# A recurrent token mixer on one NeuronCore: chunk matrices kept as 64x64 tiles without zero blocks, the triangular inverse from 16x16 blocks with two product levels, and another order of the head pairs

## The chip, the cores and the metric

The kernel runs on one core of a Trainium2 chip. The metric is device time in microseconds (us) of one execution, taken as the median of several. Durations inside the kernel come from one profiled execution; they are read in views of its trace. The engines are named as the profile names them: PE (TensorE matmuls), PEld (its weight loads), DVE (VectorE), ACT (ScalarE), POOL (GpSimd) and SP (the queue that issues DMAs).

## The reference, cut to what matters

The model is a sequence of 512 tokens, width 1024, through ffn1, a token mixer, ffn2 and two more layers. The change touches only the mixer, whose recurrence over time has one 64x64 state per head (8 heads):

```
def wkv7_scan(r, w, k, v, a, b):
    def step(S, inp):
        r_t, w_t, k_t, v_t, a_t, b_t = inp
        sa = jnp.einsum("bhvk,bhk->bhv", S, a_t)
        S = S * w_t[:, :, None, :] + sa[..., None] * b_t[:, :, None, :] + v_t[..., None] * k_t[:, :, None, :]
        y = jnp.einsum("bhvk,bhk->bhv", S, r_t)
        return S, y
...
y = wkv7_scan(rh, heads(decay), kh, vh, -kk, kk * ah)
```

Around it stand projections (`h @ w_in`, in 42 column groups of 128), three small low-rank products (`tanh(xw) @ w_decay_up`, `xa @ w_iclr_up`, `sigmoid(xg) @ w_gate_up`), a short convolution branch, a normalisation of `y` per head, and gated output projections.

## The kernel before, in words

Everything large is a `gemm`: a weight group of 128x1024 is loaded (`raw`), split into a high part `wh` (ACT or DVE) and a low part `wl` (DVE, or loaded from DRAM where ffn1 made it ahead, `put_low`), and multiplied as three products (`mm3`: high x high, high x low, low x high) of 128x128 by 128x512 in fp32r. One group with 8 row tiles is 24 such matmuls into one PSUM tile `pm`.

The recurrence is computed in 8 chunks of 64 tokens. Two heads make a pair; there are four pairs, `pair(j)` for the preparation and `pair_out(j)` for the rest. In the trace the small fp32 matmuls stand as two instructions each and write PSUM tiles named `pw`. The steps for one pair:

- `pair` makes the scaled vectors: `AR` (tile `ar`) holds the a-like and r-like vectors, `BK` (tile `bk`) the b-like and k-like ones. Its three low-rank products read `lora`; the first two use 64 rows of the array each.
- `chunk_ab`: for each of two halves (`tp`) 4 matmuls of 64x128 by 128 columns give a 128x128 matrix in which two chunks' 64x64 blocks stand on the diagonal and the rest is masked to zero with `mS` (`ab`).
- `inverse32`: the inverse of identity minus a strictly triangular 64x64 matrix is found by substitution on its 32x32 diagonal blocks, all at once on DVE: the blocks go through DRAM (`dab`) so that each lands on a partition (`n`), 31 steps of a multiply (`q`, in one or two instructions) and a reduce (into `u`), then back through DRAM (`dtt`) to `TT`.
- `batch` (once for each half): `x` (16 matmuls of 64x64 by 64 columns) and `y` (4 of 64x128 by 128); 6 fp32 transposes; one product level for the off-diagonal 32x32 block (`p1`, `p2`, 8 matmuls of 32x32 each, with `ab` and `TN` in their names); `pd` and `pq` (4 each of 128x128 by 128, `R,TN` and `R,ak`); `pm` (8 of 64x64 by 128 and 8 by 64, `R,aT` and `vT,R`).
- the scan over chunks: six steps, each with two matmuls (`zb,MN`) and two DVE adds into `zb`, a 128x128 state tile with zero blocks; and the outputs `py`: 16 matmuls by 64 columns (`vT,R`) and 7 of 128x64 by 128 (`zb,aT`), all in one PSUM bank.
- normalisation, four transposes, and two POOL products to `yo`.

The order of work is made by a list scheduler (`Rec.schedule`) from modelled costs (`_cost`). It takes the ready operation with the lowest place in the program first, looks up to 800 operations ahead, and on PE it prefers operations of the array shape in use (`choose`): an operation that needs another shape may wait while operations of the same shape are ready within 400 places, up to 3000 ns. The order found is fixed: each engine runs its list. Eight PSUM banks serve all of it, 76 slots of 128x512 hold activations, and 3, 4 and 4 buffers hold `raw`, `wh` and `wl`. At the end of the mixer `w_out_b` needs the results `ys` of all four pairs.

Almost every operation is emitted from one line (551), so views are read by tile names. The functions that the change touches:

Of the kernel before, what the change touches and what calls it, by code (L numbers as in the profile page):

```python
# [17 lines left out]
_PI = 128 * 128 + 128  # L18


def _mats(t, tp):

    return bass.AP(tensor=t.tensor, offset=t.offset + 4 * tp * _PI, ap=[[128, 128], [_PI, 4], [1, 128]])


def _diag(t, r0, nr):

    return bass.AP(tensor=t.tensor, offset=t.offset + r0 * 128, ap=[[32 * 128 + 32, 32], [128, nr], [1, 32]])
# [40 lines left out]
_CST = ["ident", "ones", "bones", "mS", "mST"]  # L69
# [3 lines left out]
_COFF["e32"] = _COFF["mI"] + 64  # L73
_COFF["eps"] = _COFF["e32"] + 256
# [4 lines left out]
def _const_block():  # L79
# [8 lines left out]
        "mS": same & (p < q),  # L88
        "mST": same & (q < p),
# [5 lines left out]
    c[:, _COFF["e32"]:_COFF["e32"] + 256] = np.repeat(np.eye(32).reshape(4, 256), 32, 0)  # L95
# [44 lines left out]
def layout(i):  # L140
# [13 lines left out]
    lo = np.stack([np.concatenate([f("w_decay_up")[0], f("w_iclr_up")[0]], 0), f("w_gate_up")[0]], 1)  # L154
    o["lora"] = np.ascontiguousarray(lo)
# [438 lines left out]
def _cost(o, outs, ins):  # L594
# [4 lines left out]
    if o.eng == "tensor":  # L599
        if o.fn == "matmul":  # L600
# [7 lines left out]
            if not one and m <= 64 and k <= 64:  # L608
                c *= 0.55
        else:  # L610
            o.mode = 128, 128
            c = 60.0
# [31 lines left out]
class Net:  # L644
# [63 lines left out]
    def D(self, p):  # L708

        t = self.rec.tile(self.dp.tile([8, _PI], F32, name=self.nm(p)), "dram", 99, True)  # L710
        return t
# [195 lines left out]
    def _mixer(self):  # L907
# [20 lines left out]
        self.lw = self.wload(self.a["lora"], (128, 2, 512))  # L928


        zero = self.T(shape=(128, 4, 128), p="z")
# [3 lines left out]
        for i in range(2):  # L935
            for tp in range(2):
                nc.sync.dma_start(out=_mats(self.dtt[i], tp), in_=zero)
# [55 lines left out]
        self.pair_out(*p.pop(1))  # L993
        p[3] = pair(3)
# [3 lines left out]
        gates(1, 5)  # L998
        self.pair_out(*p.pop(3))
        gates(5, 8)  # L1000
# [17 lines left out]
    def pair(self, j, rF, kF, vF):  # L1018
# [6 lines left out]
        lwh, lwl = self.lw  # L1025
        cols = slice(j * 128, j * 128 + 128)
        pw = self.P()
        self.mm3(pw, lwh[0:64, 0, cols], lwl[0:64, 0, cols], self.tw[0][0:64], self.tw[1][0:64], True, True)
# [3 lines left out]
        self.mm3(pa, lwh[64:128, 0, cols], lwl[64:128, 0, cols], self.tw[0][64:128], self.tw[1][64:128], True, True)  # L1032
# [3 lines left out]
        self.mm3(pg, lwh[:, 1, cols], lwl[:, 1, cols], self.sg[0], self.sg[1], True, True)  # L1036
# [46 lines left out]
        ab = [self.chunk_ab(AR[tp], BK[tp]) for tp in range(2)]  # L1083
        TTs = self.inverse32(ab, j)
        return j, AR, BK, F, vF, ab, TTs, bon, gF

    def pair_out(self, j, AR, BK, F, vF, ab, TTs, bon, gF):
# [22 lines left out]


        zb = [self.T(shape=(128, 4, 128), p="zb") for _ in range(2)]
        for z in zb:
            G.memset(z, 0.0)
        zc = lambda c: zb[c // 4][:, c % 4]
        st = []
        for tp in range(2):
            st.append(self.batch(AR[tp], BK[tp], BH, dF, vT, tp, ab[tp], TTs[tp]))
        for tp in range(2):
            MT, N, _, _ = st[tp]  # L1120
            for c in range(4):
                cc = 4 * tp + c
                if cc == 7:
                    break
                if cc == 0:
                    for hh in range(2):
                        r = slice(hh * 64, hh * 64 + 64)
                        A.copy(zc(1)[r, r], N[r, 0])
                    continue
                pz = self.W((128, 64))  # L1130
                for hh in range(2):
                    r = slice(hh * 64, hh * 64 + 64)
                    PE.matmul(pz[r], MT[r, c], zc(cc)[r, r], start=True, stop=True)
                for hh in range(2):
                    r = slice(hh * 64, hh * 64 + 64)
                    V.tensor_tensor(zc(cc + 1)[r, r], pz[r], N[r, c], ALU.add)

        py = self.W((128, 4, 128))
        for tp in range(2):
            _, _, QG, Rh = st[tp]  # L1140
            for tt in range(2):
                t = 2 * tp + tt
                for c in range(2):
                    r = slice(c * 64, c * 64 + 64)
                    last = t == 0 and c == 0
                    for hh in range(2):
                        PE.matmul(py[r, t, hh * 64:hh * 64 + 64], QG[hh][r, 1, tt, 0:64],
                                  vT[r, t, hh * 64:hh * 64 + 64], start=hh == 0, stop=last and hh == 1)
                    if not last:
                        PE.matmul(py[r, t], Rh[:, tt, c * 64:c * 64 + 64], zc(2 * t + c), start=False, stop=True)  # L1150

        yv = py.rearrange("p a (h i) -> p (a h) i", h=2)
# [27 lines left out]
        self.ys.append(self.split(o))  # L1180

    def chunk_ab(self, AR, BK):

        V, PE = self.nc.vector, self.nc.tensor
        X = [self.W((128, 2, 128)) for _ in range(2)]
        for tt in range(2):
# [608 lines left out]
```

## Time and profile before

| what | us |
|---|---|
| median of 3 runs | 1911.29 (1911.15 to 1913.51) |
| the profiled execution, its own time | 1912.9 |
| its span, first to last instruction | 1911.1 |
| PE busy in the span | 1867.3 |
| DVE busy in the span | 1334.9 |
| ACT busy in the span | 852.7 |
| POOL busy in the span | 252.5 |

The span is what the trace covers; the profiled execution's own time is 1.8 us longer. PE's busy time counts each matmul from its start to a modelled end, and neighbouring matmuls overlap, so the pace of PE is read from the starts of neighbouring matmuls and not from their durations. The mixer lies between 380 and 800 us from the span's start.

### The profile page before, as it was taken

Reading aid. Unit: us, or ns where it says so; the run is one execution under the profiler, and the core shown is the slowest. Engines: PE = TensorE matmul, PEld = TensorE weight load, DVE = VectorE, ACT = ScalarE, POOL = GpSimd, SP = SyncE. Lnnn points to the kernel's source line nnn. Section 1 sums busy time; section 2 is a strip of 40 time slices with the busy share of each in tenths; the row PEclk is TensorE's granted clock in tenths of the full one; section 3 lists DMA queues with packets and bytes.
Section 4 is the critical chain, followed back from the end, with each engine's and each line's share of the span. In section 5 each row is a group of like instructions: output and inputs, shape, how many; then the busy total and the mean of one; then the engine's idle time right before and its main releaser. Section 6 shows DMA issues by size and latency. Waiting matters only on the chain.

```text
span 1911.1 us, 25539 instructions
## 1 busy us (share of the span) xinstructions
PE 1867.3 (98%) x9756; PEld 1548.5 (81%) x9756; DVE 1334.9 (70%) x2173; ACT 852.7 (45%) x1187; POOL 252.5 (13%) x201
## 2 busy tenths in 40 slices
PE   8999999999999999999999999999999999999998
PEld 6878888878877777788788788788899888888887
DVE  7766655568977873567566567865378985899774
ACT  5333423453333422444334334522245554898671
POOL 3101101212121200411001014220000101000001
PEclk9999999999999999999999999999999999999999
DMA  7898884526633533658878774412221225555552
GB/s 257 280 318 287 303 281 158 150 97 203 190 125 111 157 129 118 221 180 297 284 262 295 271 272 131 127 58 73 84 86 45 67 67 198 184 185 204 198 176 100
DMA packets 128810, 345.36 MB, mean 181 GB/s; under 512 B 32304, under 2 KB 44848, under 8 KB 128688
## 3 DMA queue, kind: packets, MB, share of 16 engines
q1 hardware_dynamic: 128688, 343.74, 53.7%
q8 instruction: 76, 1.25, 0.3%
q14 instruction: 46, 0.38, 0.1%
HBM read 280.25 MB, written 63.44 MB: 180 GB/s over the span
## 4 chain that ended last, share of the span: by engine, by line
PE 71%; DVE 11%; DMA 11%; ACT 3%; issue 2%; POOL 1%; SPq 1%; DVEq 0%; ACTq 0%; POOLq 0%
PE pm L551 67%; DVE wl L551 4%; PE pw L551 4%; DMA low<-wl 3%; DMA raw<-o_in 2%; DVE t L551 2%; ACT wh L551 2%; DMA raw<-ffn_d 1%; DMA raw<-ffn_u 1%; DMA raw<-w_in 1%; DVE l L551 1%; DMA n<-dab 1%; DMA raw<-gw 1%; SPq L551 1%; DVE q L551 1%
## 5 line engine op out<-in xcount | busy, mean ns | idle before, releaser
L551 ACT CAST wh<-raw 128x1024 fp32r<-128x1024 f32 (+1 forms) x334 | 347.2, 1041 | 678.6 <-PE pm L551 300.7
L551 PE MATMUL pm<-xh,wh 128*128 128x512 f32 x1488 | 584.0, 393 | 9.6 <-ACT xh L551 8.0
L551 PE MATMUL pm<-xl,wh 128*128 128x512 f32 x1488 | 584.1, 393 | 1.9 <-DVE xl L551 1.9
L551 PE MATMUL pm<-xh,wl 128*128 128x512 f32 x1488 | 582.6, 392 | 1.8 <-DVE wl L551 1.8
L551 DVE TENSOR_TENSOR wl<-raw,wh 128x1024 fp32r<-128x1024 f32 (+1 forms) x303 | 383.0, 1266 | 212.1 <-DMA low<-wl 103.6
L551 PEld LDWEIGHTS pm<-xh,wh 128*128 128x128 f32 x1488 | 280.3, 189 | 69.2 <-ACT xh L551 9.1
L551 PE MATMUL pm<-h,wh 128*128 128x512 f32 (+1 forms) x844 | 321.5, 385 | 10.0 <-ACT h L551 6.8
L551 PEld LDWEIGHTS pm<-xl,wh 128*128 128x128 f32 x1488 | 280.5, 188 | 62.4 <-DVE xl L551 5.0
L551 PEld LDWEIGHTS pm<-xh,wl 128*128 128x128 f32 x1488 | 280.4, 188 | 61.6 <-DVE wl L551 4.3
L551 PE MATMUL pm<-l,wh 128*128 128x512 f32 (+1 forms) x844 | 322.2, 384 | 2.6 <-DVE l L551 2.5
L551 PE MATMUL pm<-h,wl 128*128 128x512 f32 (+1 forms) x844 | 321.4, 383 | 0.0
L551 POOL TENSOR_TENSOR t<-t,t 128x512 f32<-128x512 f32 x61 | 95.2, 1561 | 942.2 <-DVE t L551 796.1
L551 PEld LDWEIGHTS pm<-h,wh 128*128 128x128 f32 x844 | 158.2, 188 | 44.3 <-ACT h L551 8.5
L551 PEld LDWEIGHTS pm<-l,wh 128*128 128x128 f32 x844 | 158.4, 188 | 36.5 <-DVE l L551 6.5
L551 PEld LDWEIGHTS pm<-h,wl 128*128 128x128 f32 x844 | 158.5, 188 | 29.8
L551 DVE TENSOR_TENSOR t<-pm,rstd 128x512 f32<-128x512 f32 x146 | 98.7, 684 | 19.8 <-PE pm L551 15.8
L551 ACT ACT_TABLE_LOAD x71 | 91.1, 1283 | 21.9 <-DVE s L551 14.9
L551 DVE CAST wh<-raw 128x1024 fp32r<-128x1024 f32 x75 | 54.9, 733 | 50.6 <-PE pm L551 28.7
L551 POOL TENSOR_TENSOR acc<-acc,sq 128x512 f32<-128x512 f32 x42 | 65.6, 1569 | 138.5 <-ACT sq L551 138.1
L551 DVE TENSOR_TENSOR x<-x,pm 128x512 f32<-128x512 f32 (+1 forms) x44 | 27.8, 636 | 68.8 <-PE pm L551 67.3
L551 ACT ACTIVATE t<-t 128x512 f32<-128x512 f32 x100 | 59.8, 626 | 30.5 <-DVE t L551 29.5
L551 DVE TENSOR_TENSOR l<-t,h 128x512 fp32r<-128x512 f32 x84 | 58.7, 706 | 6.3 <-ACT h L551 5.0
(245 smaller groups left out, 2127.5 us busy)
## 6 DMA issues: line engine op xcount, KB each, us to landing
low<-wl SPq DMA_DIRECT2D x106, 512.0 KB, 3.8
wl<-low SPq DMA_DIRECT2D x106, 512.0 KB, 3.7
raw<-w_in SPq DMA_DIRECT2D x76, 512.0 KB, 4.8
raw<-o_in SPq DMA_DIRECT2D x64, 512.0 KB, 4.5
raw<-ffn_g SPq DMA_DIRECT2D x44, 512.0 KB, 4.0
raw<-ffn_u SPq DMA_DIRECT2D x44, 512.0 KB, 5.0
raw<-ffn_d SPq DMA_DIRECT2D x32, 512.0 KB, 5.2
raw<-o_out SPq DMA_DIRECT2D x32, 512.0 KB, 4.6
```

The source lines that it names most:

```text
L551: o.ins = getattr(getattr(self.nc, o.eng), o.fn)(*o.args, **o.kw)
```

## The change

It does this in the mixer; the rest of the program is the same text.

- All chunk matrices become 64x64 tiles: `ab`, `TT`, `TN` are 128 x 8 x 64 (chunk parity on the partition half), without zero blocks. `chunk_ab` has 16 matmuls of 64x64 by 64, `batch` 48 for `x` and `y`, 16 + 16 by 128 for `pd` and `pq`; `batch` treats both halves in one call, stage by stage.
- The substitution runs on 16x16 blocks (`inverse16`): 15 steps, each with one multiply and one reduce; half the DMAs.
- `inverse64` makes the rest with two product levels, each 16 + 16 matmuls of 64x64 by 64, with three 32x32-block transposes of 128x512 on DVE in all, and two copies on ACT.
- The state `zb` is 128 x 8 x 64, so a scan step has one add of 128x64. The outputs go to two PSUM tiles, one for each head: 16 matmuls ahead of the scan, 14 behind it, all 64x64 by 64 columns.
- The low-rank weights are padded to 128 rows, loaded in three pieces and kept in activation slots, no longer in a `wh` and a `wl` buffer.
- The order is pair 0, pair 1, conv 0, pair 2, conv 1, conv 2, out of pair 0, conv 3, pair 3, and so on; four gates stand behind the last `pair_out` in place of three.
- In the scheduler's model a fp32 matmul of 64x64 costs 31 ns (up to 64 columns) or 105 ns, and a transpose 109 ns in place of 60 ns.

```
+_CH = 64 * 64 + 64
...
+            if not one and m <= 64 and k <= 64:
+                c = 31.0 if n <= 64 else 105.0
...
-            c = 60.0
+            c = 109.0
...
-        self.lw = self.wload(self.a["lora"], (128, 2, 512))
+        self.lw = []
+        for i in range(3):
+            raw = self.T()
+            nc.sync.dma_start(out=raw, in_=self.a["lora"][i])
+            self.lw.append(self.split(raw))
...
+        p[0] = pair(0)
+        p[1] = pair(1)
         conv(0)
-        p[0] = pair(0)
+        p[2] = pair(2)
         conv(1)
-        p[1] = pair(1)
         conv(2)
+        self.pair_out(*p.pop(0))
         conv(3)
+        p[3] = pair(3)
         out_a(0)
-        self.pair_out(*p.pop(0))
-        p[2] = pair(2)
-        gates(0, 1)
+        self.pair_out(*p.pop(1))
         out_a(1)
-        self.pair_out(*p.pop(1))
-        p[3] = pair(3)
         out_a(2)
         self.pair_out(*p.pop(2))
         out_a(3)
-        gates(1, 5)
+        gates(0, 4)
         self.pair_out(*p.pop(3))
-        gates(5, 8)
+        gates(4, 8)
...
+        py = [self.W((128, 4, 64)) for _ in range(2)]
+        for t in range(4):
+            for hh in range(2):
                 for c in range(2):
                     r = slice(c * 64, c * 64 + 64)
+                    o = PE.matmul(py[hh][r, t], st[t // 2][2][hh][r, 1, t % 2, 0:64], vT[r, t, hh * 64:hh * 64 + 64],
+                                  start=t == 0, stop=False)
...
+            for hh in range(2):
+                r = slice(hh * 64, hh * 64 + 64)
+                PE.matmul(pz[r], MT[r, c], zb[r, cc], start=True, stop=True).deps.append(o)
+            V.tensor_tensor(zb[:, cc + 1], pz, N[:, c], ALU.add)
+        for cc in (2, 1, 3, 4, 5, 6, 7):
+            t, c = cc // 2, cc % 2
+            for hh in range(2):
+                r = slice(hh * 64, hh * 64 + 64)
+                PE.matmul(py[hh][c * 64:c * 64 + 64, t], st[t // 2][3][r, t % 2, c * 64:c * 64 + 64],
+                          zb[r, cc], start=False, stop=cc > 5)
...
+        for t in range(1, 16):
             p = q[:, 0:8 * t + 8].rearrange("p (r k) -> p r k", r=8)
+            V.tensor_tensor(p, U[:, :, 0:t + 1], n[:, t:t + 1, 0:t + 1].to_broadcast([128, 8, t + 1]), ALU.mult)
             V.tensor_reduce(U[:, :, t:t + 1].rearrange("p r o -> p (r o)"), p, axis=AX.X, op=ALU.add)
...
+    def inverse64(self, ab, TT):
...
+        a16 = self.T(shape=(128, 8, 64), p="a16")
+        nc.tt(a16, ab, self.c("m16", 64).unsqueeze(1).to_broadcast([128, 8, 64]), ALU.mult)
+        for lvl in range(2):
+
+            b = ab if lvl else a16
+            T = self.T(shape=(128, 8, 64), p="TN")
+            V.transpose(out=f(T), in_=f(TT))
+            p1 = self.W((128, 8, 64))
+            for m in range(8):
+                for c in range(2):
+                    k = slice(64 * c, 64 * c + 64)
+                    PE.matmul(p1[k, m], b[k, m], TT[k, m], start=True, stop=True)
+            x1 = self.T(shape=(128, 8, 64), p="XT")
+            A.copy(x1, p1)
+            p2 = self.W((128, 8, 64))
+            for m in range(8):
+                for c in range(2):
+                    k = slice(64 * c, 64 * c + 64)
+                    PE.matmul(p2[k, m], x1[k, m], T[k, m], start=True, stop=True)
...
+            else:
+                V.tensor_tensor(T, T, p2, ALU.add)
+                TT = self.T(shape=(128, 8, 64), p="TT")
+                V.transpose(out=f(TT), in_=f(T))
...
+        for tp in range(2):
+            pd = self.W((128, 4, 128))
+            for hh in range(2):
+                for tt in range(2):
+                    q = 2 * hh + tt
+                    for cc in range(2):
+                        PE.matmul(pd[sl(cc), q], T[sl(cc), 4 * tp + q], RR[tp][hh][sl(cc), 0, tt], start=True, stop=True)
...
+            pm = [self.W((128, 2, 192)) for _ in range(2)]
+            for tt in range(2):
+                for hh, cc in q4:
+                    R = RR[tp][hh]
+                    PE.matmul(pm[cc][sl(hh), tt, 0:128], aT[tp][sl(cc), 0, tt, sl(hh)], R[sl(cc), 0, tt], start=True, stop=True)
```

## Rows read from the trace of the kernel before

**Rows 1.** Part 1 of the page: busy time of PE, PEld, DVE and ACT over the span, share, and number of instructions.

```profile
PE 1867.3 (98%) x9756; PEld 1548.5 (81%) x9756; DVE 1334.9 (70%) x2173; ACT 852.7 (45%) x1187; POOL 252.5 (13%) x201
```

**Rows 2.** Busy time by stretch (us from the span's start): length, then busy us and instructions of PE, PEld, DVE, ACT, POOL, then the granted share of PE's clock, the DMA share and GB/s. The last row is the whole mixer.

```profile
440.00:500.00 60.00, 59.32 (x282) 47.96 (x280) 52.47 (x139) 16.59 (x20) 15.96 (x15) 1.00 0.64 194
...
620.00:680.00 60.00, 55.78 (x497) 43.16 (x497) 52.34 (x141) 27.38 (x47) 13.76 (x15) 1.00 0.47 143
680.00:740.00 60.00, 60.00 (x463) 48.10 (x460) 37.19 (x104) 16.25 (x34) 2.58 (x2) 1.00 0.43 143
740.00:800.00 60.00, 56.75 (x268) 42.55 (x267) 27.66 (x48) 20.56 (x28) 16.20 (x11) 1.00 0.49 179
380.00:800.00 420.00, 406.35 (x2705) 320.61 (x2704) 308.82 (x745) 157.04 (x253) 78.61 (x76) 1.00 0.47 151
```

**Rows 3.** The same view for PE alone and for the matmuls of the `pm` tiles alone, over the mixer: length, busy us, number of matmul instructions, clock, DMA share, GB/s.

```profile
380.00:800.00 420.00, 320.34 (x1321) 1.00 0.47 151
```

**Rows 4.** The same for the `pw` tiles (all the small fp32 matmuls and transposes).

```profile
380.00:800.00 420.00, 98.04 (x1384) 1.00 0.47 151
```

**Rows 5.** Timeline of PE, a run of large matmuls one behind the other: start, duration, what. The first and the ninth of nine neighbours.

```profile
460.69 0.39 PE L551 MATMUL pm<-xh,wh 128*128 128x512 f32 x1
...
462.50 0.39 PE L551 MATMUL pm<-xh,wl 128*128 128x512 f32 x1
```

**Rows 6.** Timeline of PE, stretch 518 to 520.5 us: `x` of one half, two times `y`, then the two low-rank products with 64 rows (from 519.36 up to the next `x`).

```profile
518.21 0.76 PE L551 MATMUL pw<-ar,bk 64*64 64x64 f32 x32
518.89 0.72 PE L551 MATMUL pw<-bk,ar 64*128 64x128 f32 x8
519.36 0.48 PE L551 MATMUL pm<-h,wh 64*128 64x512 f32 x2
...
520.24 0.47 PE L551 MATMUL pw<-ar,bk 64*64 64x64 f32 x15
```

**Rows 7.** Timeline of PE, single transposes at 521.6 us, and the start of the next one.

```profile
521.51 0.27 PE L551 MATMUL pw<-cst,bh 128*128 128x128 f32 x1
521.62 0.27 PE L551 MATMUL pw<-cst,kh 128*128 128x128 f32 x1
```

**Rows 8.** Timeline of PE, stretch 533 to 537 us: one product of the inverse (8 matmuls of 32x32), and six matmuls of `pd`.

```profile
533.13 0.69 PE L551 MATMUL pw<-XT,TT 32*32 32x32 f32 x16
533.75 0.50 PE L551 MATMUL pm<-xh,wh 128*128 128x512 f32 x1
...
535.02 1.50 PE L551 MATMUL pw<-R,TN 128*128 128x128 f32 x12
536.35 1.06 PE L551 MATMUL pw<-R,ak 128*128 128x128 f32 x8
```

**Rows 9.** Timeline of PE, part of `pm` at 540 us: groups of two matmuls by 128 columns and two by 64.

```profile
540.15 0.43 PE L551 MATMUL pw<-R,aT 64*64 64x128 f32 x4
540.37 0.33 PE L551 MATMUL pw<-vT,R 64*64 64x64 f32 x4
540.53 0.43 PE L551 MATMUL pw<-R,aT 64*64 64x128 f32 x4
```

**Rows 10.** Timeline of PE, one step of the scan at 547 us, between two large matmuls.

```profile
547.09 0.39 PE L551 MATMUL pm<-xh,wh 128*128 128x512 f32 x1
547.41 0.33 PE L551 MATMUL pw<-zb,MN 64*64 64x64 f32 x4
547.67 0.43 PE L551 MATMUL pw<-zb,aT 128*64 128x128 f32 x2
548.03 0.44 PE L551 MATMUL pw<-vT,R 64*64 64x64 f32 x4
548.41 0.50 PE L551 MATMUL pm<-xl,wh 128*128 128x512 f32 x1
548.74 0.39 PE L551 MATMUL pm<-xh,wl 128*128 128x512 f32 x1
```

**Rows 11.** DVE over the mixer, groups by form (busy us, mean ns of one, idle before): the multiply of the substitution at 128 and at 16 elements a partition, the reduce at 128, and the block transpose.

```profile
L551 DVE TENSOR_TENSOR q<-u,n 128x128 f32<-128x128 f32 x72 | 29.4, 412 | 0.9
...
L551 DVE STREAM_TRANSPOSE TN<-TT 128x512 f32<-128x512 f32 x8 | 5.5, 700 | 0.1
...
L551 DVE TENSOR_TENSOR q<-u,n 128x16 f32<-128x16 f32 x8 | 1.6, 206 | 0.0
...
L551 DVE TENSOR_REDUCE u<-q 128x8 f32<-128x128 f32 x4 | 1.2, 289 | 0.0
```

**Rows 12.** Busy time of DVE over the mixer for the instructions that write or read `u` (the whole substitution): length, busy us, count.

```profile
380.00:800.00 420.00, 91.97 (x314) 1.00 0.47 151
```

**Rows 13.** The longest entry of the waits of PE over the mixer: us in total, times, longest.

```profile
PE pm L551 <- DVE wl L551: 1.8, 4, 1.0
```

**Rows 14.** The chain that ended last, in order of time, last part of the mixer: start, length, what, number of instructions.

```profile
749.15 1.00 PE pw L551 x10
750.15 3.18 PE pm L551 x13
...
762.26 6.36 PE pm L551 x27
768.62 0.45 PE pw L551 x4
...
772.63 2.94 issue
```

More of the change, by code (lines that the diff above doesn't have):

```diff
@@ L935, in _mixer @@
         for i in range(2):
[L936 to L937 removed]
+            for c in range(2):
+                nc.sync.dma_start(out=_mats(self.dtt[i], c), in_=zero[64 * c:64 * c + 64])
         self.ys = []
@@ L1082, in pair, with pair_out @@
         V.tensor_tensor(bon, vF, pb, ALU.mult)
[L1083 to L1087, printed above, removed]
+        ab = self.chunk_ab(AR, BK)
+        TT = self.inverse16(ab, j)
+        return j, AR, BK, F, vF, ab, TT, bon, gF
+    def pair_out(self, j, AR, BK, F, vF, ab, TT, bon, gF):
         nc = self.nc
@@ L1109, in pair_out @@
         A.copy(vT, pv)
[L1112 to L1142, printed above, removed]
+        st = self.batch(AR, BK, BH, dF, vT, ab, TT)
+        py = [self.W((128, 4, 64)) for _ in range(2)]
+        for t in range(4):
+            for hh in range(2):
                 for c in range(2):
                     r = slice(c * 64, c * 64 + 64)
[L1145 to L1150, printed above, removed]
@@ L1272, in batch @@
-        T = self.T(shape=(128, 4, 128), p="TN")
-        V.transpose(out=T.rearrange("p a i -> p (a i)"), in_=TT.rearrange("p a i -> p (a i)"))
-        p1 = self.W((128, 4, 32))
-        p2 = self.W((128, 4, 32))
-        x1 = self.T(p="XT")[:, 0:128].rearrange("p (q i) -> p q i", q=4)
-        for b in (0, 64):
-            lo, up = slice(b, b + 32), slice(b + 32, b + 64)
-            for q in range(4):
-                PE.matmul(p1[up, q], ab[lo, q, up], T[lo, q, lo], start=True, stop=True)
-            A.copy(x1[up], p1[up])
@@ L1292, in batch @@
-        for hh in range(2):
-            pq = self.W((128, 2, 128))
-            for tt in range(2):
-                PE.matmul(pq[:, tt], ak[:, 2 * hh + tt], RR[hh][:, 0, tt], start=True, stop=True)
-            V.tensor_tensor(RR[hh][:, 1], RR[hh][:, 1], pq, ALU.add)
-        MN = self.T(shape=(128, 2, 4, 64), p="MN")
-        MT, N = MN[:, 0], MN[:, 1]
+        q4 = [(hh, cc) for hh, cc in ((0, 0), (1, 1), (0, 1), (1, 0))]
+        sl = lambda i: slice(i * 64, i * 64 + 64)
+        mI = self.c("mI", 64).unsqueeze(1).to_broadcast([128, 4, 64])
@@ new lines, in batch @@
+        for tp in range(2):
+            pa = self.W((128, 2, 128))
+            pb = self.W((128, 2, 2, 128))
+            for tt in range(2):
+                t = 2 * tp + tt
+                PE.transpose(pa[:, tt], AR[tp][:, tt, 0], self.ident)
+                for i in range(2):
+                    PE.transpose(pb[:, i, tt], BH[i][:, t * 128:(t + 1) * 128], self.ident)
+            t = self.T(shape=(128, 2, 2, 128), p="aT")
+            A.copy(t[:, 0], pa)
+            aT.append(t)
+            for hh in range(2):
+                A.copy(RR[tp][hh][:, :, :, 64:128], pb[:, :, :, hh * 64:hh * 64 + 64])
@@ new lines, in batch @@
+        T = self.inverse64(ab, TT)
+        for tp in range(2):
+            pd = self.W((128, 4, 128))
+            for hh in range(2):
+                for tt in range(2):
+                    q = 2 * hh + tt
+                    for cc in range(2):
+                        PE.matmul(pd[sl(cc), q], T[sl(cc), 4 * tp + q], RR[tp][hh][sl(cc), 0, tt], start=True, stop=True)
+            for hh in range(2):
+                A.copy(RR[tp][hh][:, 0], pd[:, 2 * hh:2 * hh + 2])
+        for tp in range(2):
+            pq = self.W((128, 4, 128))
+            for hh in range(2):
+                for tt in range(2):
+                    q = 2 * hh + tt
+                    for cc in range(2):
+                        PE.matmul(pq[sl(cc), q], ak[tp][sl(cc), q], RR[tp][hh][sl(cc), 0, tt], start=True, stop=True)
+            for hh in range(2):
+                V.tensor_tensor(RR[tp][hh][:, 1], RR[tp][hh][:, 1], pq[:, 2 * hh:2 * hh + 2], ALU.add)
```

215 lines of the change are left out of this document (102 added, 113 removed).

## The prediction

> **What bounds the kernel now.** I read the page's busy times first: PE is busy for 1867.3 of 1911.1 us, DVE for 1334.9 [rows 1]. Matmul records overlap, so that share says only that PE is seldom without work; its pace comes from the timeline. Nine large matmuls in a row start 0.226 us apart (462.50 - 460.69 = 1.81 us over eight) [rows 5]. Then the stretches: in the mixer, 380 to 800 us, PE is busy for 406.35 of 420 us, so it waits for 13.65 us; the clock is granted in full (1.00, the 2.4 GHz level) in every stretch shown [rows 2]. The largest entry among PE's waits sums to 1.8 us over four of them [rows 13]. DVE is close behind, 52.47 of 60 us at 440 to 500, but PE is still busy there for 59.32 [rows 2]. So the mixer is bound by what PE issues, and a change is worth the PE time that it takes out, less the waits that it adds.
>
> How PE's 420 us divide: 1321 large matmuls [rows 3] at 0.226 are 298.5 us. The other 121.5 us go to the 1384 small instructions [rows 4], the passages between array shapes, and the 13.65 us of waits. The records of the small ones cover 98.04 us [rows 4]; since they overlap with the large ones, I cost them by starts instead.
>
> **The small matmuls before, for one pair.** (A small fp32 matmul is two instructions.)
> - 20 transposes at 0.11 [rows 7]: 2.2 us.
> - `x`: 32 instructions from 518.21 to 518.89, 0.69 us, two times: 1.4. This is all four 64x64 tiles of the array at work: 0.043 us a matmul.
> - `y` and `ab`, 16 matmuls of 64x128: four take 0.47 (518.89 to 519.36) [rows 6], so 1.9.
> - the inverse's four products: 0.62 each (533.13 to 533.75) [rows 8]: 2.5.
> - `pd` and `pq`, 16 matmuls: six in 1.33 (535.02 to 536.35) [rows 8], 0.222 each: 3.55.
> - `pm`: eight groups of 0.38 [rows 9]: 3.0.
> - the scan: six steps of 1.00 (547.41 to 548.41), which hold 12 of the 16 first output products; four more at 0.11 and one `zb,aT` at 0.36 [rows 10]: 6.8.
>
> Sum 21.3, four pairs 85.4. With the waits that leaves 121.5 - 85.4 - 13.65 = 22.4 us for passages between shapes.
>
> **After, for one pair.** One row decides much of it. In a scan step the two `zb,MN` matmuls (heads 0 and 1, so different rows and different columns of the array) end 0.33 us after their first start; two matmuls on one tile (`vT,R`) need 0.44 [rows 10]. The 0.11 missing are two instruction times of 0.055: diagonal tiles run side by side, although both write the one bank of `pz`. So 64 columns cost 0.11 a matmul on one tile, 0.055 on two, 0.0275 to 0.043 on four.
> - transposes: 2.2.
> - `ab`, `x`, `y`: 64 on four tiles, taken at 0.043 [rows 6] (bounds 0.0275 and 0.055): 2.75.
> - `inverse64`: 64 matmuls, always on the two diagonal tiles, 0.055: 3.5.
> - `pd`, `pq`: 32 by 128 columns on two tiles, half of 0.222 [rows 8]: 3.55, as before.
> - `pm`: the matmuls of before on four tiles in place of two; half of 3.0: 1.5 (bounds 1.5 and 3.0).
> - scan: six times 0.26 (547.41 to 547.67) [rows 10]: 1.55.
> - outputs: 16 on diagonal tiles at 0.055 and 14 on four at 0.043: 1.5.
>
> Sum 16.55. The difference, 4.75 a pair, is **19.0 us**: the inverse becomes 1 us dearer, the scan with its outputs 3.75 cheaper, `pm` 1.5, and the rest of it is the 64x128 form.
>
> **Passages.** Around a scan step the large matmul ahead of it takes 0.32 and the one behind it 0.33 in place of 0.226 [rows 10]: 0.20 us a burst. After the change I count 16 bursts a pair (`ab`, `x` with `y`, four products, `pd`, `pq`, `pm`, six steps, last outputs), 64 x 0.20 = 12.8 if none merges, against 22.4. But the scan's 24 bursts stay, two products are new, `pd` and `pq` leave the shape of the large ones, and part of the 22.4 is the first slow instruction of a burst, which stays. Bounds 0 and -9.6; I take **-3**, nearer to none.
>
> **The low-rank products.** Two products on half the rows took 0.88 us (519.36 to 520.24) [rows 6]; on full rows six instructions at 0.226 take 1.36: **+1.9** for four pairs. The weight buffers that they held become free; that can only shorten waits.
>
> **Off the path.** DVE spends 91.97 us on the substitution [rows 12]. Fifteen steps of a multiply between 0.206 and 0.412 and a reduce up to 0.289 [rows 11] are at most 10.5 a pair, 42 in all, so DVE loses 50 us or more; the third transpose (0.70 [rows 11]), the full-width add (also some 0.7) and the masked copy give back 2 a pair, the single add a scan step returns about as much. PE waits hardly at all for DVE, so this is worth at most what is left of the 13.65. ACT's two copies of 512 elements take the place of four small ones; ACT is busy for 157 of 420 us [rows 2]. SP issues 8 DMAs a pair where it issued 16, of half the size. POOL loses two memsets. If DVE had no room, the 2 us a pair would come back as waits of `TN`'s readers, 8 us.
>
> **Order.** The eight weight groups without a premade low part are needed at the start in both orders, so DVE splits the same. Pairs 0 to 2 are prepared before the first `pair_out`. Nothing is priced here; what hides the chains is the 3.18 us of large matmuls between scan steps [rows 14], and where that runs out the third rival's price holds. The new transpose cost also moves operations in the later layers: 3 us either way in the range.
>
> **Sum.** -19.0 - 3 + 1.9 = -20.1, with waits unchanged. Against the profiled execution's own 1912.9 that is 1892.8; the median of the runs shown is 1.6 lower, so 1891.
>
> **Rivals.**
> - *More comes back.* Bursts merge (-6.6 beyond my 3), all four-tile work runs at 0.0275 (-4.8), and with DVE free PE's waits fall by half (-7): 1891 - 18 = 1873. For it: DVE at 52.34 of 60 in 620 to 680, just where PE has 4.2 us of its waits [rows 2]. Against: no one wait is long.
> - *PE time turns into waits.* The work goes as said, but the rows saved lay where PE would wait for the chain anyhow; `pm` stays at 3.0 (+6) and waits take 12 to 14: 1910. For it: at the end, 740 to 800, PE already waits for 3.25 us [rows 2] and the chain leaves PE for POOL [rows 14].
> - *The longer chain, slower than before.* Each `pair_out` gains two dependent PE products and two transposes. A scan step now comes round every 4.18 us, 1.00 of it small and 3.18 large matmuls that go first [rows 14]; two more turns, 1.4 of transposes and 0.7 of add are 10.5 us a pair. While there are large matmuls to issue this costs nothing. For the last pair the cover is four gates of 24 x 0.226 = 5.4 us and what `w_out_b` can do with three pairs in the banks left (the two output tiles and one of the scan take three of eight). If only that pair is uncovered, 1901, in my range; it decides from two uncovered pairs on (21 us against 20.1), and with all four it is 1891 + 42 = 1933. Against: PE had no wait at all from 680 to 740 [rows 2], and the last pair's preparation moves ahead of all four `out_a`.
> - *Row tiles that share a bank take turns.* Then diagonal products run one behind the other: 3.5 for `inverse64`, 3.55 for `pd` and `pq`, 0.9 for outputs, 7.95 a pair, 31.8: 1923, slower. The rows speak against it (0.33 and 0.44 above) for two matmuls; for 16 in a row nothing is shown. The Trainium skill has this rule, in TensorEngine Tiling (Array Packing), Restrictions and Gotchas: different row tiles cannot use the same PSUM bank at one time. By that rule the 1923 holds; the trace disagrees in the scan step, where both tiles of `pz` lie in one bank.
>
> **Chances.** Forecast (1880 to 1902) 0.6; more comes back 0.2; turned into waits 0.08; longer chain 0.08; one bank 0.04. The range leaves out the two slow cases and a little of the first: it goes from 1869 (low bounds of every part) to 1910 (`pm` at 3.0, +6; four-tile work at 0.055, +3.2; no passages saved, +3; waits +5; later layers +2). A measurement of this kernel can tell about 0.2%, 3.8 us, from no change. Faster by more 0.81, same 0.08, slower 0.11.
>
> **What would show it.** Right: `x` and `y` of a half within about 1.0 us, a product of `inverse64` (16 matmuls) in 0.9 us, `pm` of a half in 0.75, a scan step in 0.26 with no `zb,aT` behind it, the mixer about 20 us shorter with PE's waits near 13. Wrong: products of 1.8 us (one bank), PE waits over 25 us in the mixer (chain), a granted clock of 0.5 in a stretch with many small matmuls, or ffn2 beginning with waits that the mixer gave away.

## The result and the profile after

The changed kernel takes **1883.11 us** (median of 4 runs, 1879.47 to 1883.99) where the kernel before, on the same chip, takes 1912.40 (1911.15 to 1916.64, 4 runs): a ratio of 0.984, 95% interval 0.983 to 0.986. The forecast was 1891, the range 1869 to 1910. The profiled execution took 1883.26 us, its span is 1881.5. The saving is 29 us instead of 20, and the two parts that make it up are both further from the forecast than that: in the profiled executions the mixer became 38.8 us shorter, and 9.4 us were lost outside it.

Part 1 of the page of after [rows 1]:

```profile
PE 1842.7 (98%) x10324; PEld 1540.2 (82%) x10324; DVE 1272.1 (68%) x1956; ACT 852.2 (45%) x1180; POOL 246.4 (13%) x193
```

Busy time by stretch of after, columns as in [rows 2]; the last row is the whole mixer, which now ends near 793 us instead of 825, so that 386 to 769 holds about as many large matmuls as 380 to 800 did:

```profile
506.00:566.00 60.00, 60.00 (x749) 49.61 (x748) 35.50 (x88) 18.46 (x34) 5.55 (x6) 1.00 0.49 167
...
686.00:746.00 60.00, 60.00 (x443) 48.53 (x442) 18.68 (x47) 19.05 (x35) 6.49 (x5) 1.00 0.36 120
...
386.00:769.00 383.00, 377.81 (x3281) 309.61 (x3280) 241.65 (x521) 159.09 (x247) 77.69 (x69) 1.00 0.48 155
```

The same view for three tiles: `pm` on PE, `pw` on PE, and `u` (the substitution) on DVE:

```profile
386.00:769.00 383.00, 314.59 (x1329) 1.00 0.48 155
386.00:769.00 383.00, 70.08 (x1952) 1.00 0.48 155
386.00:769.00 383.00, 33.13 (x121) 1.00 0.48 155
```

PE is idle for 5.19 us of the 383 where it was idle for 13.65 of 420 [rows 2]. There are 1329 large matmuls where there were 1321 [rows 3]. The 1384 small instructions became 1952, but their records cover 70.08 us, not 98.04 [rows 4]. DVE's substitution went from 91.97 [rows 12] to 33.13 us.

The timeline of PE of after, from different pairs: one product of `inverse64`, `pd` and `pq`, `pm` with the output products behind it, one scan step.

```profile
510.99 1.15 PE L555 MATMUL pw<-TT,a 64*64 64x64 f32 x32
512.07 0.50 PE L555 MATMUL pm<-xh,wh 128*128 128x512 f32 x1
...
529.54 1.96 PE L555 MATMUL pw<-R,TN 64*64 64x128 f32 x32
531.34 1.80 PE L555 MATMUL pw<-R,ak 64*64 64x128 f32 x30
...
593.13 0.33 PE L555 MATMUL pw<-R,aT 64*64 64x128 f32 x2
...
594.77 1.19 PE L555 MATMUL pw<-vT,R 64*64 64x64 f32 x38
595.76 0.22 PE L555 MATMUL pw<-zb,MN 64*64 64x64 f32 x1
...
706.55 0.27 PE L555 MATMUL pw<-zb,MN 64*64 64x64 f32 x2
706.57 0.27 PE L555 MATMUL pw<-zb,aT 64*64 64x64 f32 x2
706.65 0.23 PE L555 MATMUL pw<-zb,MN 64*64 64x64 f32 x2
706.67 0.32 PE L555 MATMUL pw<-zb,aT 64*64 64x64 f32 x6
706.93 0.50 PE L555 MATMUL pm<-xh,wl 128*128 128x512 f32 x1
```

A product of 16 matmuls takes 1.08 us from its first start to the next large matmul (512.07 - 510.99), `pd` 1.80 (531.34 - 529.54), `pm` of both halves, with the last of `pq` in it, 1.64 (594.77 - 593.13). A scan step takes 0.38 us (706.93 - 706.55), and the output products `zb,aT` run inside those 0.38, on the tiles that `zb,MN` leaves free. PE never leaves the small shape between `pd`, `pq`, `pm` and the first scan step.

The longest waits of PE of after, 386 to 770 us [rows 13]:

```profile
PE pm L555 <- ACT h L555: 1.5, 1, 1.5
PE pm L555 <- DMA wl<-low: 1.2, 1, 1.2
PE pm L555 <- DVE wl L555: 1.0, 1, 1.0
```

The chain that ended last, of after, at the scan of the last pair [rows 14]: small steps of 0.38, and 15 or 16 large matmuls between them.

```profile
706.62 0.38 PE pw L555 x12
707.00 3.63 PE pm L555 x15
...
711.00 3.85 PE pm L555 x16
```

**Where the time went.** I split both traces by the large matmuls (the first and the last of the mixer) and summed, from one start to the next on PE, the small instructions and what the large ones took beyond 0.2267 us each.

| us | before | after | difference |
|---|---|---|---|
| up to the mixer (ffn1) | 383.7 | 390.0 | +6.3 |
| mixer | 441.5 | 402.7 | -38.8 |
| of it small instructions by starts | 97.4 | 68.3 | -29.1 |
| of it excess on the large ones | 23.6 | 13.9 | -9.7 |
| (PE's waits, in these two) | 13.7 | 5.2 | -8.5 |
| after the mixer | 1078.6 | 1081.7 | +3.1 |

Counted the same way, the shape of PE's tile changes 171 times in the mixer before and 62 times after, and 59 separate bursts of small work became 37. Three things make up the 38.8 us. PE's waits are 8.5 of them. Another 1.7 come from the clock: 3.4 us of the mixer before stand at half clock (a granted clock of 0.5, the 1.2 GHz level), none after. The remaining 28.6 us are work: small instructions and excess without the waits and without what half clock adds were 105.6 us and are 77.0.

**ffn1**, which the diff doesn't touch, is 6.3 us longer. Waits of PE of after, 0 to 390 us, without the long one at the start (before has 1.6 and 0.9 us in these two); then PE by stretch (length, busy us and matmuls, granted clock, DMA share, GB/s):

```profile
PE pm L555 <- ACT h L555: 3.1, 2, 1.9
PE pm L555 <- DVE xl L555: 1.6, 2, 1.2
```

```profile
106.00:110.00 4.00, 1.90 (x8) 0.98 0.91 315
110.00:117.00 7.00, 6.56 (x16) 0.53 0.87 302
```

PE waits for 2.1 of the 4 us from 106 to 110, and then the granted clock is 0.53 over 7 us (most of it at the 1.2 GHz level): 16 large matmuls, where the experiment E4 below has 32 in the same stretch.

### The profile page after: what moved, and what is told of

Read it like the earlier page. It is cut to its first block, busy times and chain, and to the rows that moved or that the text cites. A ratio compares the mean times of both kernels' runs of the same rounds, so it can differ in the third digit from the quotient of the medians.

```text
span 1881.5 us, 26365 instructions
## 1 busy us (share of the span) xinstructions
PE 1842.7 (98%) x10324; PEld 1540.2 (82%) x10324; DVE 1272.1 (68%) x1956; ACT 852.2 (45%) x1180; POOL 246.4 (13%) x193
## 4 chain that ended last, share of the span: by engine, by line
PE 73%; DMA 11%; DVE 11%; ACT 3%; issue 2%; POOL 0%; SPq 0%; DVEq 0%; ACTq 0%; POOLq 0%
PE pm L555 69%; DVE wl L555 5%; PE pw L555 4%; DMA low<-wl 2%; DMA raw<-o_in 2%; ACT wh L555 2%; DVE t L555 2%; DMA raw<-ffn_d 1%; DMA raw<-ffn_u 1%; DVE l L555 1%; DMA raw<-gw 1%; DMA raw<-w_in 1%; DMA raw<-w_out_a 1%; DVE wh L555 0%; DVE u L555 0%
## 5 line engine op out<-in xcount | busy, mean ns | idle before, releaser
L555 PEld LDWEIGHTS pm<-xh,wl 128*128 128x128 f32 x1488 | 280.2, 188 | 60.5 <-DVE wl L555 2.8
L555 POOL TENSOR_TENSOR t<-t,t 128x512 f32<-128x512 f32 x60 | 88.8, 1481 | 932.1 <-DVE t L555 712.5
L555 POOL TENSOR_TENSOR acc<-acc,sq 128x512 f32<-128x512 f32 x42 | 66.2, 1584 | 140.0 <-ACT sq L555 139.7
L555 DVE TENSOR_TENSOR x<-x,pm 128x512 f32<-128x512 f32 (+1 forms) x44 | 27.9, 637 | 72.5 <-PE pm L555 70.4
```

Source lines behind the costliest of these rows:

```text
L555: o.ins = getattr(getattr(self.nc, o.eng), o.fn)(*o.args, **o.kw)
```

## Experiments

The theories after the result. For the mixer: the passages were priced too low, and PE's waits fell because the pairs' chains got shorter; the rival was that the order of the pairs or the scheduler's new costs did it. For ffn1: the constants block got narrower (1284 instead of 1540 columns), and so the scheduler, which costs its transfer, ordered ffn1 otherwise; the rival was chance between executions. Every experiment is split like the table above; the columns small and waits overlap, since a wait ahead of a small instruction counts in both. Bursts are counted in the trace; the expectations count them in the program's order, where after has 31.

| run | us (median) | ratio to before, 95% | ffn1 | mixer | small | waits | bursts |
|---|---|---|---|---|---|---|---|
| after | 1883.1 | 0.984 [0.983, 0.986] | 390.0 | 402.7 | 68.3 | 5.2 | 37 |
| E1 old order | 1892.4 | 0.989 [0.987, 0.991] | 389.4 | 414.7 | 73.0 | 13.5 | 44 |
| E2 old costs | 1889.7 | 0.987 [0.985, 0.989] | 389.4 | 413.7 | 74.8 | 9.9 | 34 |
| E3 before, new scan | 1910.0 | 0.998 [0.997, 0.999] | 386.1 | 435.4 | 87.9 | 12.4 | 65 |
| E4 padded constants | 1872.3 | 0.978 [0.976, 0.980] | 381.3 | 402.3 | 68.0 | 4.9 | 37 |
| E5 substitution twice | 1894.5 | 0.990 [0.989, 0.992] | 387.7 | 418.7 | 80.3 | 13.1 | 38 |
| E6 two banks | 1883.5 | 0.985 [0.983, 0.986] | 387.5 | 406.5 | 70.4 | 6.8 | 38 |
| E7 no hold | 1881.6 | 0.984 [0.982, 0.986] | 385.0 | 406.6 | 72.4 | 3.1 | 55 |
| E8 old low-rank | 1885.2 | 0.985 [0.984, 0.987] | 387.3 | 410.0 | 66.8 | 8.0 | 38 |
| E9 before, new order | 1944.7 | 1.016 [1.014, 1.018] | 386.2 | 473.1 | 106.6 | 32.3 | 56 |
| E10 substitution aside | 1887.7 | 0.987 [0.985, 0.989] | 387.0 | 414.1 | 68.7 | 9.6 | 43 |
| E11 padded, longer hold | 1877.9 | 0.981 [0.980, 0.983] | 381.9 | 407.8 | 71.5 | 7.8 | 32 |

**E1, the old order of pairs** in the changed kernel.

```diff
         conv(0)
+        p[0] = pair(0)
         conv(1)
+        p[1] = pair(1)
...
+        self.pair_out(*p.pop(0))
+        p[2] = pair(2)
+        gates(0, 1)
```

> The changed kernel (1883.1 us) with the order of pairs, convolutions and gates of before. Theory: the gain is PE time of the small matmuls and of the passages between array shapes, and the order only decides how bursts merge. In this program's order on PE the small matmuls stand in 37 bursts among the large ones, in the changed kernel in 31, so about 6 x 0.2 = 1.2 us more, and waits of PE between the 5 us of the changed kernel and the 14 of before: 1884 to 1893. Rival: the order of pairs is a main part of the gain (it lets the substitution of three pairs run early): then most of the fall in waits and passages goes back, 1895 or more.

Measured 1892.4. The longest waits of PE in the mixer:

```profile
PE pm L555 <- DVE wl L555: 2.8, 2, 2.6
PE pw L555 <- DVE R L555: 2.4, 1, 2.4
```

So the order, priced at nothing in the prediction, is worth 9.2 us here, at the upper end of the theory's range. Of the 12.0 us that the mixer is longer, 8.3 are waits, 1.7 half clock, and 2.0 work, with 44 bursts in place of 37. The small instructions' own work is no dearer: their 4.7 us more are waits and half clock.

**E2, the scheduler's old costs** for small fp32 matmuls and transposes.

```diff
-                c = 31.0 if n <= 64 else 105.0
+                c *= 0.55
...
-            c = 109.0
+            c = 60.0
```

> The changed kernel with the scheduler's old costs for small matmuls and transposes. Theory: the costs move little, since in the order on PE the small matmuls stand in 30 bursts against 31: 1880 to 1888. Rival: the better costs are what removed the waits of PE; then its waits in the mixer go from 5 back to about 13 us and the time to 1891 or more.

Measured 1889.7, 6.6 us more than after, above the theory's range and below the rival's. The two numbers change no instruction, only where each stands; small work by starts is 74.8 us and the waits are 9.9. Of the 11.0 us that the mixer is longer, 4.7 are waits, 3.1 half clock and 3.2 work. The costs are a part of the gain.

**E3, the new scan and outputs alone** in the kernel before (states of 64 columns, no `zb` memsets).

```diff
-        zb = [self.T(shape=(128, 4, 128), p="zb") for _ in range(2)]
-        for z in zb:
-            G.memset(z, 0.0)
+        zb = self.T(shape=(128, 8, 64), p="zb")
...
-        py = self.W((128, 4, 128))
+        py = [self.W((128, 4, 64)) for _ in range(2)]
```

> The kernel before with one part of the change alone: states of 64 columns, one add a scan step, outputs in two PSUM tiles ahead of and behind the scan. Theory of small matmuls: a scan step falls from 1.00 us of PE to 0.26, the outputs cost 1.5 us a pair, so 3.75 us a pair less, 15 in all: 1912 - 15 = 1897, and 24 passages into the 128x64 shape and 24 out of it go as well, which is within the 1.00; range 1892 to 1900. Rival: the scan's matmuls lay beside large ones and PE only waits instead: no faster than 1908.

Measured 1910.0, 0.2% less than before, a miss: the theory had 1897. The small work did get 9.5 us cheaper (97.4 to 87.9). PE by stretch shows what took it:

```profile
556.00:568.00 12.00, 12.00 (x141) 1.00 0.54 176
568.00:580.00 12.00, 11.01 (x44) 0.72 0.28 65
752.00:764.00 12.00, 8.22 (x49) 1.00 0.00 0
764.00:772.00 8.00, 7.09 (x20) 0.57 0.00 0
```

After 3.78 us of idle time between 752 and 764 the granted clock is 0.57 over 8 us, and 0.72 over the 12 us from 568, where PE waits 0.99 us. Over the mixer 17 us stand at half clock where before had 3.4, some 7 us lost; ffn1 is 2.4 us longer. Without the 2.8 us that half clock adds to the small work itself, it got 12.3 us cheaper, of the 15 priced. The product saving is real and is mostly eaten by two things that no product's price holds.

**E4, the constants block padded** to its old width. Nothing reads the padding.

```diff
-_NC = _COFF["reset"] + 512
+_NC = _COFF["reset"] + 512 + 256
```

> The changed kernel with the block of constants padded to its size of before (1540 columns in place of 1284), nothing else. ffn1, which the change does not touch, ended 6.3 us later in the changed kernel; its program order there differs from before, because the scheduler sees a shorter load at the start. Theory: that order is what costs the 6.3 us (a wait at 107 us and a stretch of 6.8 us at the lower clock behind it); with the old size ffn1 runs as before and the time is 1876 to 1879. Rival: the stretch at the lower clock falls where it falls, whatever the order; then the time stays at 1880 to 1884.

Measured **1872.3**, the best of all and 10.9 us below after. PE by stretch, the stretch of ffn1 shown above for after:

```profile
106.00:110.00 4.00, 3.60 (x16) 1.00 0.93 308
110.00:117.00 7.00, 7.00 (x32) 1.00 0.96 337
```

The time is 3.7 us below the theory's range. ffn1 is 8.7 us shorter than in after, and PE's order in it is that of the kernel before (its first 1638 instructions are the same); the mixer is the same (402.3). So ffn1's loss came with the scheduler's order, by way of the block's width. Not all of the 8.7 us is the order, though. Eight traces have after's order on PE in ffn1 (after, E1, E2, E5 to E8, E10), and there it ends between 385.0 and 390.0 us, 387.9 in the mean, with after the longest; in E4 and E11 it ends at 381.3 and 381.9, and in before, E3 and E9, with the same order on PE, at 383.7 to 386.2. By the means of the two orders, 383.8 and 387.9, the order on PE is worth some 4 us; the rest differs between traces with the same one. That the order goes through the modelled time of the block's transfer is argued, not shown.

**E5, the substitution twice** in the chain. The second pass adds each step's sum again, so the inverse is another one; the number and form of all other instructions are the same.

```diff
-        for t in range(1, 16):
+        for t in [i for i in range(1, 16) for _ in range(2)]:
```

> The changed kernel (1883.1 us) with each of the 15 steps of the substitution done twice, with the same results: DVE's 33.13 us on it double, some 8 us more in the chain of each pair. In the changed kernel PE's waits in the mixer fell from 13.7 to 5.2 us. Theory: the order of pairs covers the chains and DVE's load is off the path: waits stay at 5 to 8 us, 1883 to 1887. Rival: the lighter DVE took the waits away: they go back to 13 or so, 1891 or more.

Measured 1894.5, with 13.1 us of waits, as the rival had it:

```profile
PE pw L555 <- DVE R L555: 4.2, 3, 3.6
PE pm L555 <- DVE wl L555: 2.0, 2, 1.7
PE pw L555 <- ACT XT L555: 1.8, 2, 1.2
```

DVE was priced at nothing because no one wait of PE for it was long. With 60.5 us of substitution in place of 33.1 (still less than the 91.97 of before), the waits are back. The longest is for an add into `R`, in another pair's chain; DVE's timeline around it:

```profile
524.03 0.25 DVE L555 TENSOR_TENSOR u<-u,n 128x88 f32<-128x88 f32 x1
...
528.49 0.26 DVE L555 TENSOR_REDUCE u<-u 128x8 f32<-128x96 f32 x1
528.78 0.42 DVE L555 TENSOR_TENSOR R<-R,pw 128x256 f32<-128x256 f32 x1
```

The product that the add takes up starts its last instructions on PE at 525.12 us; the add begins at 528.78, behind steps of the substitution and what stands between them.

**E6, each product of the inverse in two banks**, one for each row tile.

```diff
-            p1 = self.W((128, 8, 64))
+            p1 = [self.W((128, 8, 64)) for _ in range(2)]
...
-                    PE.matmul(p1[k, m], b[k, m], TT[k, m], start=True, stop=True)
+                    PE.matmul(p1[c][k, m], b[k, m], TT[k, m], start=True, stop=True)
```

> The changed kernel with the two diagonal tiles of each product of the inverse in PSUM banks of their own (and the copies and adds behind them in two halves). Theory: the tiles run side by side in one bank already, so a product of 16 matmuls takes 1.08 us as before; two more banks in use and eight more small instructions of ACT and DVE a pair cost 0 to 5 us: 1883 to 1888. Rival: sharing a bank slows the tiles; a product falls to 0.95 us or less, and the time to 1881 or less.

Measured 1883.5 against 1883.1. The timeline of PE, one product with two banks:

```profile
513.97 1.15 PE L555 MATMUL pw<-TN,XT 64*64 64x64 f32 x32
515.05 0.50 PE L555 MATMUL pm<-xh,wh 128*128 128x512 f32 x1
```

1.08 us (515.05 - 513.97), as with one bank. Row tiles in one bank don't take turns here.

**E7, small work not held back**: the scheduler no longer delays a small matmul until another of its shape can join.

```diff
-        self.near, self.wait = 400, 3000.0
+        self.near, self.wait = 400, 0.0
```

> The changed kernel with the scheduler's preference for the array shape in use taken away (a wait of 0 in place of 3000 ns). The small matmuls then stand in 55 bursts on PE in place of 31. Theory: a passage costs PE 0.2 us and merged bursts share tiles better, so 24 x 0.2 = 5 us and up to 4 more: 1887 to 1893, small matmuls by starts 70 to 74 us in place of 68. Rival: passages are hidden and the chains run faster without the hold: 1883 or less.

37 bursts became 55, the small work by starts 68.3 to 72.4, the mixer 402.7 to 406.6: 3.9 us for 18 bursts, **0.22 us a burst**, where the prediction had 0.20 from [rows 10]. But the rival's half shows too: the waits fell from 5.2 to 3.1 us. Without them the 18 bursts cost 6.0 us, **0.33 us a burst**, of which 2.8 us are on `zb,aT`, which in after ran beside `zb,MN`. The whole kernel shows nothing of it (1881.6, the rival's time): ffn1 ended at 385.0 here, with no half-clock stretch.

**E8, the old low-rank products** on half the rows, without the zeros.

```diff
-        self.mm3(pw, *lw[0], *self.tw, True, True)
+        self.mm3(pw, lwh[0:64, 0, cols], lwl[0:64, 0, cols], self.tw[0][0:64], self.tw[1][0:64], True, True)
```

> The changed kernel with the low-rank weights as before: two products on 64 rows each, weights in one high and one low weight buffer until the last pair is prepared. Theory of small matmuls: 0.88 in place of 1.36 us a pair, 1.9 less, and a passage or two more into the 64-row shape a pair, 0.2 each: 1881 to 1884. Rival: the two buffers matter, since the large matmuls then wait for weights: waits of PE in the mixer rise from 5 to 9 or more, 1887 or more.

Measured 1885.2, the mixer 7.3 us longer than in after: 8.0 us of waits, and 6.8 us in all at half clock. Putting the half-row products back brings no gain. Their own price holds: from one start to the next the 24 half-row matmuls take 1.8 us less than 24 full ones. But the waits rise by 2.8 us, half clock adds 3.4, and the rest of the work is 2.9 us dearer, with 74 shape changes in place of 62. The waits rose as the rival said, though not to its 9.

**E9, the new order alone** in the kernel before (the edit of E1 the other way round).

```diff
         conv(0)
-        p[0] = pair(0)
+        p[2] = pair(2)
         conv(1)
```

> The kernel before with the new order of pairs alone; products, substitution and states are the old ones. The old order in the changed kernel cost 9.2 us (1892.4 against 1883.1) and put PE's waits in the mixer back from 5.2 to 13.5 us. Theory, the order is worth that only where the pair's chain is short: here the substitution still takes DVE 23 us a pair (91.97 in all), so the waits stay at 11 to 14 us, the shape changes at 160 to 175, and the time at 1905 to 1914. Rival, the order by itself gives the large matmuls that hide the chain: waits of 5 to 8 us and 1899 to 1904.

Measured **1944.7**, 1.6% slower than before, and neither theory had it. One wait of PE, one of ACT, then the timelines of DVE and ACT at that place:

```profile
PE pw L551 <- ACT R L551: 17.0, 1, 17.0
```

```profile
ACT R L551 <- DVE q L551: 15.7, 1, 15.7
```

```profile
610.89 0.07 DVE L551 MEMSET n<- 128x16 f32 x1
...
634.70 0.66 DVE L551 TENSOR_TENSOR q<-u,n 128x128 f32<-128x128 f32 x2
635.39 0.42 DVE L551 TENSOR_TENSOR R<-pw,cst 128x256 f32<-128x256 f32 x1
```

```profile
635.10 0.37 ACT L551 COPY R<-pw 128x256 f32<-128x256 f32 x1 [15.70 <-DVE q L551]
```

From 610.9 to 635.4 us DVE does nearly nothing but one pair's substitution. Two things of another pair stand behind it: DVE's own mask into `R`, and ACT's copy into `R`, which computes nothing from `q` and yet is released as half of the last step's multiply ends (it starts at 634.70, takes 0.37 us, and is the last to read the first `n` tile). The cause is a buffer: in the built program all 76 slots are in use, this `R` lies at the address of that `n`, and the copy waits for the count that `n`'s last reader sets. What more slots would have given wasn't tried. PE stands for 17.0 us, and over the stretch:

```profile
621.00:649.00 28.00, 13.47 (x77) 11.66 (x78) 18.43 (x59) 3.28 (x10) 0.00 (x0) 0.51 0.14 47
```

The granted clock is 0.51 from 621 to 649. Of the 31.6 us that the mixer is longer than in before, 18.6 are waits and some 13 half clock outside the waits; the work is the same (105.9 against 105.6), and the shape changes stay (167 against 171), as the theory said. So the order by itself merges nothing. The order that is worth 9 us with a substitution of 15 steps costs 30 (1944.7 against 1914.3 of the kernel before, measured beside it) with one of 31.

**E10, a second substitution aside**, into a tile that nothing reads.

```diff
+            p = q2[:, 0:8 * i + 8].rearrange("p (r k) -> p r k", r=8)
+            V.tensor_tensor(p, U2[:, :, 0:i + 1], n[:, i:i + 1, 0:i + 1].to_broadcast([128, 8, i + 1]), ALU.mult)
```

> The changed kernel with a second substitution into a tile that nothing reads: DVE gets the same 33 us more as in the run that did the substitution twice in the chain (which came to 1894.5 us with 13.1 us of PE's waits in the mixer), but these instructions stand behind the first pass on DVE and lie in no pair's chain, except where DVE's order puts them ahead of work that PE wants. Theory, the length of the chain took the waits back: waits of 5 to 8 us, mixer 403 to 407, time 1881 to 1887. Rival, DVE's load took them back: waits of 11 to 14 us, mixer 414 to 419, time 1891 to 1896.

Measured 1887.7, between the two theories; the mixer is at the rival's 414.1, the waits (9.6) are not. The run didn't do what I had meant: the scheduler set the steps of the two passes alternately, so the records of `u` cover 40.6 us, not 66, and the first pass ends later too. Its longest wait is again a matter of DVE's order:

```profile
ACT h L555 <- DVE sh L555: 4.2, 1, 4.2
```

```profile
PE pm L555 <- ACT h L555: 4.9, 1, 4.9
```

```profile
457.00:466.00 9.00, 5.77 (x16) 0.62 0.51 135
```

The first row is a wait of ACT, the second what PE then waits for, the last PE by stretch: `sh`, from which the large matmuls' operand is made, stands behind the substitutions on DVE. Length of the chain and load of DVE aren't told apart by this pair of runs.

**E11, E4 with a hold twice as long** (`wait` 6000 in place of 3000).

> The changed kernel with the constants block padded to its old width (1872.3 us) and, in addition, small work held back for up to twice as long so that more of it goes together: in program order 28 bursts of small matmuls in place of 31. Theory, a passage costs 0.22 us and the waits have room: 3 bursts are 0.7 us, so 1870 to 1873, no difference that can be told. Rival, small work held longer comes late to its chain and to DVE: waits in the mixer rise from 4.9 to 8 us or more and the time is 1875 to 1880.

Measured 1877.9, 5.6 us more than E4. The bursts fell from 37 to 32, 1.1 us by E7's lower price (the work without waits and half clock fell by 0.3); the waits rose from 4.9 to 7.8 us, and 6.8 us of the mixer ran at half clock. The rival held, with waits just under its 8: fewer passages are worth less here than work that comes late.

## Why the prediction was right, and where it was not

- **Small matmuls, -19.0.** The pieces came out close to their price: `pd` 1.80 for 1.775, a product of the inverse 1.08 with its passage for 0.875, `pm` of a pair 1.64 for 1.5; a scan step 0.38 with its passage and output products for 0.26 without; the new scan alone (E3) gave 9.5 us of small work, 12.3 without half clock, for 15. Two diagonal tiles in one bank do run side by side. `ab`, `x` and `y` were priced at 0.043 us a matmul and, where they run as one burst, take about 0.03 (some 62 in the 1.9 us from 485.3 us). All small work after, by starts and without waits, is 66.5 us for the priced 66.2.
- **Passages, -3: the step that failed.** I took a value near "none merges", because the scan's 24 bursts stay and `pd` and `pq` leave the shape of the large ones. By the prediction's own subtraction (small by starts plus the excess, less the waits, less the sum of the pieces) they were 121.0 - 13.7 - 85.4 = 21.9 us and are 82.2 - 5.2 - 66.2 = 10.8 (the low-rank products among them): about **-11**. Without the 1.7 us of half clock, and with the 0.9 us that the low-rank products cost taken out, the passages themselves are some -10, at my lower bound of -9.6 and three times what I took. The price of a burst was about right (0.22 to 0.33 in E7), the number was not: I counted 64 bursts if none merges, the trace has 37, and the shape changes went from 171 to 62. Nearly all chunk work now has one shape, so products of one pair ride in another pair's scan steps and `zb,aT` inside its own. With the new order alone the changes stay at 167 (E9), with the new scan alone they are 128 (E3). The Trainium skill (TensorEngine Tiling (Array Packing), Key Properties) says that a change of the tiling mode drains TensorE, and gives no price; E7 agrees in that a burst costs 0.22 to 0.33 us for the way in and out.
- **Waits, 0: the other step that failed.** They fell by 8.5 us. The prediction showed the largest entry of PE's waits, 1.8 us [rows 13], and took it that PE waits hardly at all for DVE. The whole list of before for the mixer holds 13 entries for DVE and one for ACT, and the 13 add up to 12.8 us of the 13.7; the next three are:

```profile
PE pw L551 <- DVE TN L551: 1.7, 2, 0.9
PE pm L551 <- DVE l L551: 1.5, 2, 0.7
PE pm L551 <- DVE bon L551: 1.4, 1, 1.4
```

  In after the entries for DVE add up to 2.1 us, with the old order (E1) to 12.5. So nearly all the waits of before were for DVE, in many short pieces. Old order, old costs and a longer substitution each bring 4.7 to 8.3 of them back (E1, E2, E5), and the order without the short substitution adds 18.6 (E9: 32.3 for 13.7). These don't add up; it is the schedule as a whole. What E5, E9 and E10 show in their rows is a mechanism: DVE works in order, and a substitution is a block of it behind which another pair's masks, adds and buffers stand. The prediction saw that DVE was free of 50 us and more, and valued that by the one largest wait, not by the sum of them nor by who stood behind the block.
- **Low-rank products, +1.9.** Nearer +0.9: by starts and without waits, the 24 half-row matmuls of before took only 0.9 us less than 24 full ones, because two of the four pairs did not run them as fast as [rows 6]. What the freed weight buffers brought is not separable (E8).
- **Outside the mixer, 3 either way.** +9.4: ffn1 +6.3, in part by its order and in part by how these two executions fell (E4), and after the mixer +3.1, where 13.6 us stand at half clock that were 6.8. I had tied such moves to the transposes' cost and had not thought of a block's width.
- **The rivals.** "More comes back" describes the mixer (its 1873 is what E4 gives, 1872.3). "PE time turns into waits" and the longer chain didn't happen: PE has no idle time from 506 to 566 or 686 to 746. "Row tiles that share a bank take turns" is refuted by the 1.08 us of after and E6. By the rule of the Trainium skill (TensorEngine Tiling (Array Packing), Restrictions and Gotchas) 16 such matmuls would have run one behind the other; the measurement disagrees.

So the number held by luck, because two errors of opposite sign met: the mixer gave 18.7 us more than forecast (8.5 of waits and most of the rest from the passages), the rest took 9.4. Of the signs that were to show it right, the products came near; a mixer about 20 us shorter with waits near 13 did not.

What stays open: how much of the fall of the waits is the shorter chain, how much the shorter block on DVE and how much the buffers that come free sooner; and by which of its costs the scheduler reorders ffn1 when the constants block gets narrower.

## What to carry to other kernels

Giving small products one common shape is worth more than the time of the products alone: count the shape changes that vanish, and which work can then ride in which burst, beside the instructions. Before calling an engine free, add up all the waits for it: here the largest was 1.8 us and the sum 12.8. Ask of an in-order engine off the critical path how long its longest unbroken block is and whose work stands behind it; an order of work that is good with a short block can be far worse with a long one. And where a scheduler sets the order, compare the stages that the change does not touch, in more than one trace: here a padding of 256 unused columns was worth 11 us.

## What the runs showed of the hardware

- The same stretch of program doesn't always get the same clock. ffn1 is the same sequence on PE, DVE and ACT in after, E6 and E7. In all three PE stands for 2.1 to 2.5 of the 4 us from 106 us; over the next 7 us the granted clock was 0.53 in after, and in E6 and E7:

```profile
110.00:117.00 7.00, 6.73 (x23) 0.76 0.92 318
```

```profile
110.00:117.00 7.00, 7.00 (x31) 1.00 0.96 335
```

  ffn1 ended at 390.0, 387.5 and 385.0 us.
- A wait can cost more than its length. In E9 a wait of 17.0 us stands in 28 us at a granted clock of 0.51, and in E10 the clock is 0.62 over the 9 us in which a wait of 4.9 us ends.
- Products on diagonal 64x64 tiles take the same 1.08 us for 16 whether both tiles write one bank or two.
